# The complex product behind the scans moved from VectorE to GpSimd, with two output products a tile in place of four

## The chip, the core and the metric

The kernel runs on one core of a Trainium2 chip. Its engines work side by side, each from its own queue and in order: TensorE (PE in the profile; PEld is its loading of weights), VectorE (DVE), ScalarE (ACT), GpSimd (POOL) and SyncE (SP), which here issues most of the transfers. Engines wait for each other by semaphores. The metric is the device time of one execution in microseconds. Before the change it is 2902.01 us, the median of three runs (2901.09 to 2902.54).

## The reference

The model has two blocks. The change touches one branch of the second, a state space layer of 512 channels in 32 groups of 16, with 64 complex states in each group, over 512 tokens:

```python
def s5_branch(u, a_re, a_im, log_step, b_re, b_im, c_re, c_im, d_skip, w_glu):
    ...
    xr = jnp.einsum('blgh,gph->blgp', ug, br)
    xi = jnp.einsum('blgh,gph->blgp', ug, bi)
    ...
    _, _, sr, si = lax.associative_scan(_complex_affine_combine, (lr, li, xr, xi), axis=1)
    y = (jnp.einsum('blgp,ghp->blgh', sr, c_re.astype(f32))
         - jnp.einsum('blgp,ghp->blgh', si, c_im.astype(f32)))
    y = y.reshape(bsz, seq, SSM_WIDTH) + d_skip.astype(f32) * u32
    y = jax.nn.gelu(y).astype(u.dtype)
    ...
```

Each state obeys s[t] = lambda s[t-1] + x[t] with a complex lambda. The second branch of the same block is a forgetting attention of 8 heads; both end in the same output projection.

## The kernel before, in words

All 512 tokens lie along the free axis. The 32 groups x 64 states make 2048 states, which are 16 tiles of 128 partitions by 512 tokens; here they are called tile 0 to tile 15. The complex recurrence is done with two real scans. With lambda = mag e^(i theta), the states are first turned by e^(-i theta t), then scanned with the real factor mag, then turned back by e^(i theta t). The turning factors cos and sin are the tile `e` (halves `er` and `ei`), which SyncE loads for each state tile from HBM (L1034).

For each tile `s5_x` does this: TensorE multiplies the channels with the input matrices into two PSUM tiles (L1042, `pmm<-uT,BT`); VectorE turns them with four products that read PSUM and two sums (`w1`, `w2`, `t`); two scans follow (L1064 on `w1`, L1065 on `w2`); and four more VectorE products give er*w1, ei*w2, er*w2 and ei*w1 (`sr`, `p`, and `w2` and `w1` in place). All element operations written through the helper `tt` stand as L1056 in the profile. `s5_y` multiplies each of the four with an output matrix (L1082, `CD`; the differences are in the signs of `CD`), accumulating 32 output channels in one quarter of a PSUM tile. Tiles s and s-1 write different quarters, and their products are issued in turn. After four tiles VectorE adds the skip term (L1088).

`s5_step` runs once or twice in each half turn of the loop over pairs of attention heads: it does the output products of the tile before, then the next tile's input side, then issues the load of the next `e`. Between the steps stand the attention's projections (weights are loaded by SyncE, L108, and split into two parts by ScalarE, L114, and VectorE, L115), its norms (L1134, `qf`, and the split into `qh` and `ql`, L144 and L145), its scores (L1166 to L1170), its transposes (L1183) and the product with the values, which ends in L1203. The order on each engine comes from a scheduler, which takes instructions from different parts as they are expected to be ready; so a VectorE queue holds pieces of attention and of the state space branch in turn, and it is fixed before the run. A buffer that is reused makes its next writer wait for its last reader: `w1` and `w2` have three buffers, `sr`, `p` and `t` one, `e` two.

GpSimd has nothing to do in this part of the kernel; elsewhere it adds squares (L160), multiplies in the routing (L1467) and gathers rows.

Of the kernel before, what the change touches and what calls it, by code (L numbers as in the profile page):

```python
# [9 lines left out]
F32 = mybir.dt.float32  # L10
# [6 lines left out]
OP = mybir.AluOpType  # L17
# [54 lines left out]
def tile_kernel(ctx: ExitStack, tc: tile.TileContext, I, out, dump=None, stop=None):  # L72
    nc = tc.nc
# [10 lines left out]
    def P(name, i=None, n=1):  # L84
        o, c = _POFF[name]
        return par[:, o:o + c] if i is None else par[:, o + i:o + i + n]
# [101 lines left out]
    def scaled_split(wk, pr, g, x, hi, lo, n, bias=None):  # L188
# [4 lines left out]
        else:  # L193
# [13 lines left out]
                            in1=P("cc").rearrange("p (k t) -> p k t", t=2), op=OP.mult)  # L207
# [255 lines left out]
    for h in range(5):  # L463
# [6 lines left out]
        if h < 3:  # L470
            n = 2 * (h + 2)
# [22 lines left out]
    def tmp(bufs=3, tag="tmp", dt=F32):  # L494
        return p2.tile([128, T], dt, name=tag, tag=tag, bufs=bufs)

    def psm():
        return ps.tile([128, T], F32, name="pmm", tag="mm")
# [140 lines left out]
    for n in range(10):  # L639
        pr = psm()  # L640
        proj(pr, "w_rg", n, *hx)
        u = tmp(tag="u", bufs=3)
# [23 lines left out]
    for c in range(8):  # L666
        pu = psm()
        proj(pu, "w_u", c, *hx)
        u = tmp(tag="u", bufs=3)
        nc.scalar.activation(u, pu, GELU)  # L670
        pss = psm()
        for n in range(4):
            nc.tensor.matmul(pss[:, n * 128:(n + 1) * 128], v[n][:, c * 128:(c + 1) * 128], wst[:, c],
                             start=True, stop=True)
        y = tmp()
        nc.vector.tensor_tensor(out=y.rearrange("p (n q) -> p n q", n=4),
                                in0=pss.rearrange("p (n q) -> p n q", n=4),
                                in1=bsb[:, c:c + 1].to_broadcast([128, 4, 128]), op=OP.add)
# [7 lines left out]
    for d in range(KT):  # L686
        s5_go(N_GG)
        if d % 2 == 0:
            t = midp.tile([128, D], F32, name="thg", tag="v", bufs=4)
# [8 lines left out]
    for d in range(KT):  # L698
        pp = psm()
        proj(pp, "w_pg", d, col(ygh, 8), col(ygl, 8))  # L700
        y = tmp()
# [27 lines left out]
    s5x = ctx.enter_context(ExitStack())  # L729
    s5p = s5x.enter_context(tc.tile_pool(name="s5p", bufs=1, side="right", reuse_waits="tile"))  # L730
    BT = [s5p.tile([128, 4, 128], F32, name=f"BT{i}") for i in range(2)]
    CD = [s5p.tile([128, 16, 32], F32, name=f"CD{i}") for i in range(3)]

    def s5_mats(nc, wk):
        def tt(o, a, b, op):
            nc.vector.tensor_tensor(out=o, in0=a, in1=b, op=op)

        b1 = wk.tile([128, 16, 16], F32, name="b1")
        b2 = wk.tile([128, 16, 16], F32, name="b2")

        bre = wk.tile([128, 16, 16], F32, name="bre")
        bim = wk.tile([128, 16, 16], F32, name="bim")
        nc.scalar.dma_start(bre, I["b_re"])
        nc.scalar.dma_start(bim, I["b_im"])
        BD = [wk.tile([128, 16, 32], F32, name=f"BD{i}") for i in range(2)]
        _, cr, ci = S5C
        crb = cr.rearrange("p (s o) -> p s o", o=1).to_broadcast([128, 16, 16])
        cib = ci.rearrange("p (s o) -> p s o", o=1).to_broadcast([128, 16, 16])
        for i, (xa, xb, op) in enumerate(((bre, bim, OP.subtract), (bim, bre, OP.add))):
            nc.vector.memset(BD[i], 0.0)  # L750
            tt(b1, xa, crb, OP.mult)
            tt(b2, xb, cib, OP.mult)
            for hf in range(2):
                sl = slice(64 * hf, 64 * hf + 64)
                tt(BD[i][sl, :, 16 * hf:16 * hf + 16], b1[sl], b2[sl], op)
        cc = [wk.tile([128, 16, 16], F32, name=f"cc{i}") for i in range(2)]
        for i, n in enumerate(("c_re", "c_im")):
            nc.scalar.dma_start(cc[i], I[n])
            nc.vector.memset(CD[i], 0.0)
            for hf in range(2):  # L760
                sl = slice(64 * hf, 64 * hf + 64)
                nc.vector.tensor_scalar(CD[i][sl, :, 16 * hf:16 * hf + 16], cc[i][sl], (1.0, -1.0)[i], None, op0=OP.mult)
        nc.vector.tensor_scalar(CD[2], CD[0], -1.0, None, op0=OP.mult)
        return BD

    def s5_bt(BD, psp):
# [84 lines left out]
    o = ffn_g(0)  # L851
    for j in range(22):
        o2 = ffn_g(j + 1) if j < 21 else None
        ffn_v(j, o)
        o = o2
# [170 lines left out]
    S5 = {"n": 0, "sp": sx.enter_context(tc.tile_pool(name="sp", bufs=1, side="right", reuse_waits="tile"))}  # L1026
# [5 lines left out]
    def s5_e(s):  # L1032
        e = S5["sp"].tile([128, 2, T], F32, name="e", tag="e", bufs=2)
        nc.sync.dma_start(e.rearrange("p i t -> p (i t)"), Ed[s])  # L1034
        S5["e", s] = e[:, 0], e[:, 1]

    def s5_in(s, c):

        q, i = divmod(s, 4)
        rows = slice(32 * i, 32 * i + 32)  # L1040
        px = S5["x", s, c] = psm()
        nc.tensor.matmul(px, BT[c][rows, q], uT[rows, q], start=True, stop=True)  # L1042

    def s5_x(s):


        if s == 0:
            s5_in(0, 0)
        s5_in(s, 1)
        if s < 15:  # L1050
            s5_in(s + 1, 0)
        pxr, pxi = S5.pop(("x", s, 0)), S5.pop(("x", s, 1))
        f = lambda n, b=1: S5["sp"].tile([128, T], F32, name=n, tag=n, bufs=b)
        er, ei = S5.pop(("e", s))
        sr, t, w1, w2 = f("sr"), f("t2"), f("w1", 3), f("w2", 3)
        tt = lambda o, x, y, op: nc.vector.tensor_tensor(out=o, in0=x, in1=y, op=op)  # L1056
        tt(w1, er, pxr, OP.mult)
        tt(t, ei, pxi, OP.mult)
        tt(w1, w1, t, OP.add)
        tt(w2, er, pxi, OP.mult)  # L1060
        tt(t, ei, pxr, OP.mult)
        tt(w2, w2, t, OP.subtract)
        mb = S5C[0][:, s:s + 1].to_broadcast([128, T])
        nc.vector.tensor_tensor_scan(out=w1, data0=mb, data1=w1, initial=0.0, op0=OP.mult, op1=OP.add)  # L1064
        nc.vector.tensor_tensor_scan(out=w2, data0=mb, data1=w2, initial=0.0, op0=OP.mult, op1=OP.add)  # L1065
        p = f("p2")
        tt(sr, er, w1, OP.mult)
        tt(p, ei, w2, OP.mult)
        tt(w2, er, w2, OP.mult)
        tt(w1, ei, w1, OP.mult)  # L1070
        S5["s", s] = (sr, p, w2, w1)

    def s5_y(s):


        for n in range(2):
            for u, j in ((s, n), (s - 1, 2 + n)):
                if 0 <= u < 16:
                    q, i = divmod(u, 4)
                    if i == 0 and j == 0:  # L1080
                        S5["py", q] = psm()
                    nc.tensor.matmul(S5["py", q][32 * i:32 * i + 32], CD[(0, 2, 1, 1)[j]][:, u], S5["s", u][j],  # L1082
                                     start=j == 0, stop=j == 3)
        if s > 0:
            del S5["s", s - 1]
        q, i = divmod(s - 1, 4)
        if s > 0 and i == 3:
            nc.vector.scalar_tensor_tensor(yT[:, q], uT[:, q], P("ssm_d", q), S5.pop(("py", q)), op0=OP.mult, op1=OP.add)  # L1088

    def s5_step():  # L1090
        s = S5["n"]
        if s > 17:
            return
        if s > 0:
            s5_y(s - 1)
        if s < 16:
            s5_x(s)
        if s < 15:
            s5_e(s + 1)
        S5["n"] = s + 1  # L1100
# [130 lines left out]
    for i in range(4):  # L1231
        p = a_scores(2 * i, QK[0], QK[2])
# [12 lines left out]
        p = a_scores(2 * i + 1, QK[1], QK[3])  # L1245
# [13 lines left out]
        if i < 3:  # L1259
            v_ = a_v(i + 1)  # L1260
            QK = a_norm2(raw, rs)
            s5_step()
    while S5["n"] <= 17:
        s5_step()
    ax.close()
    dump("ys5", yT)
# [16 lines left out]
    for d in range(KT):  # L1283
        wh, wl = load_w(I["w_glu"][d].rearrange("p g k c -> p (g k c)"))
        pp = []
        for g in range(2):
            pz = psm()
            for k in range(4):
                s = slice((4 * g + k) * 128, (4 * g + k) * 128 + 128)
# [356 lines left out]
    for jg in range(NB // AJ):  # L1646
# [11 lines left out]
        for jj in range(AJ):  # L1658
            j = AJ * jg + jj
# [48 lines left out]
    for n in range(NB):  # L1708
        while len(due) < 3 and n + len(due) < NB:
            due.append(v_in(n + len(due)))  # L1710
        if 56 <= n < 56 + 8 * NTD and n % 8 == 0:
            t = n // 8 - 7
# [109 lines left out]
```

## Time and profile before

| | |
|---|---|
| median of three runs | 2902.01 us |
| the profiled execution | 2902.67 us |
| its span in the trace | 2900.9 us |
| TensorE busy | 2793.5 us, 96% |
| VectorE busy | 1976.4 us, 68% |
| ScalarE busy | 1157.0 us, 40% |
| GpSimd busy | 448.0 us, 15% |

The trace's times count from the start of the span; 1.8 us of the execution lie outside it. Busy time of TensorE is modelled, and matmuls overlap, so the distance between the starts of two matmuls says more than the duration of one. The state space tiles run from 1058 us (first input product) to 1378 us (last sum).

In the rows below, a row of the timeline has the start in us, the duration in us, the engine, the line and operation, output and inputs with their shapes, the number of instructions merged into the row, and, in brackets, how long the engine stood idle before and what ended it. A row of the groups has the number of instructions, their busy time in us and the mean of one in ns. A row of busy time by stretch has its bounds and length, then the busy us (and instructions) of PE, PEld, DVE, ACT and POOL, the granted clock, the share of the DMA engines and GB/s. A float32 product of L1082 or L1042 leaves two rows in the trace.

### The profile page before, as it was taken

Reading aid. Unit: us, or ns where it says so; the run is one execution under the profiler, and the core shown is the slowest. Engines: PE = TensorE matmul, PEld = TensorE weight load, DVE = VectorE, ACT = ScalarE, POOL = GpSimd, SP = SyncE. Lnnn points to the kernel's source line nnn. Section 1 sums busy time; section 2 is a strip of 40 time slices with the busy share of each in tenths; the row PEclk is TensorE's granted clock in tenths of the full one; section 3 lists DMA queues with packets and bytes.
Section 4 is the critical chain, followed back from the end, with each engine's and each line's share of the span. In section 5 each row is a group of like instructions: output and inputs, shape, how many; then the busy total and the mean of one; then the engine's idle time right before and its main releaser. Section 6 shows DMA issues by size and latency. Waiting matters only on the chain.

```text
span 2900.9 us, 37769 instructions
## 1 busy us (share of the span) xinstructions
PE 2793.5 (96%) x14335; PEld 2274.1 (78%) x14335; DVE 1976.4 (68%) x3569; ACT 1157.0 (40%) x1597; POOL 448.0 (15%) x470
## 2 busy tenths in 40 slices
PE   7999999999999999999999979999989999999999
PEld 4777888877888876666788879999989977777776
DVE  6786894348777686886448999998765444444444
ACT  4666523233323333434434335555543333333332
POOL 1000000010000010000000054555433122222220
PEclk9999999999999999999999989999999999999999
DMA  6333363333333332222223268989887678888884
GB/s 246 121 110 109 99 192 110 120 104 120 94 92 97 88 129 80 88 77 69 95 95 117 81 229 290 339 302 345 318 328 252 223 274 302 315 304 317 310 309 161
DMA packets 167623, 540.16 MB, mean 186 GB/s; under 512 B 16912, under 2 KB 42128, under 8 KB 163984
## 3 DMA queue, kind: packets, MB, share of 16 engines
q1 hardware_dynamic: 128272, 391.94, 40.2%
q0 software_dynamic: 36864, 134.23, 12.6%
q10 hardware_dynamic: 2304, 11.57, 1.1%
q8 instruction: 112, 1.84, 0.3%
q14 instruction: 71, 0.58, 0.1%
HBM read 479.48 MB, written 58.20 MB: 185 GB/s over the span
## 4 chain that ended last, share of the span: by engine, by line
PE 80%; DVE 9%; issue 4%; POOL 2%; ACT 2%; DMA 2%; DVEq 0%; POOLq 0%; SPq 0%; ACTq 0%
PE acc L1721 19%; PE pmm L122 16%; PE pmm L123 16%; PE pmm L124 16%; PE accg L1598 2%; DVE wlo L115 2%; POOL rows L1552 2%; DMA rows<-in_peer_u_rows_dram,idx 1%; PE pm L217 1%; PE pmm L1082 1%; PE pg L122 1%; PE pg L123 1%; PE pg L124 1%; DVE rows L1563 1%; ACT whi L114 1%
## 5 line engine op out<-in xcount | busy, mean ns | idle before, releaser
L114 ACT ACTIVATE whi<-raw 128x1024 fp32r<-128x1024 f32 (+2 forms) x502 | 517.9, 1032 | 900.4 <-PE pmm L123 724.4
L115 DVE TENSOR_TENSOR wlo<-raw,whi 128x1024 fp32r<-128x1024 f32 (+2 forms) x502 | 607.9, 1212 | 307.1 <-ACT whi L114 302.5
L124 PE MATMUL pmm<-nph,wlo 128*128 128x384 f32 (+1 forms) x1152 | 398.1, 346 | 21.5 <-DVE wlo L115 21.5
L122 PE MATMUL pmm<-nph,whi 128*128 128x384 f32 (+1 forms) x1152 | 404.8, 352 | 0.3 <-ACT whi L114 0.3
L123 PE MATMUL pmm<-npl,whi 128*128 128x384 f32 (+1 forms) x1152 | 396.9, 345 | 0.0
L145 DVE TENSOR_TENSOR wtl<-w,wth 128x384 fp32r<-128x384 f32 x128 | 71.3, 559 | 294.7 <-ACT wth L144 294.7
L1721 PE MATMUL acc<-whi,wth 128*128 128x512 f32 x768 | 244.7, 399 | 0.3 <-DVE idxT L1577 0.3
L124 PEld LDWEIGHTS pmm<-nph,wlo 128*128 128x128 f32 x1152 | 219.7, 191 | 31.3 <-DVE wlo L115 26.0
L1721 PE MATMUL acc<-wlo,wth 128*128 128x512 f32 x768 | 241.8, 396 | 0.0
L1721 PE MATMUL acc<-whi,wtl 128*128 128x512 f32 x768 | 241.2, 395 | 0.0
L144 ACT ACTIVATE wth<-w 128x384 fp32r<-128x384 f32 x128 | 67.1, 525 | 397.3 <-PE acc L1721 387.2
L122 PEld LDWEIGHTS pmm<-nph,whi 128*128 128x128 f32 x1152 | 220.3, 191 | 5.1 <-ACT whi L114 0.6
L123 PEld LDWEIGHTS pmm<-npl,whi 128*128 128x128 f32 x1152 | 220.0, 191 | 4.9 <-DVE npl L145 0.3
L1552 POOL DMA_INDIRECT rows<-in_peer_v_rows_dram,idxT x128 | 125.6, 981 | 505.2 <-PE accg L1598 402.3
L1563 DVE SCALAR_TENSOR_TENSOR rows<-rows,hN 128x1024 f32<-128x1024 f32 x128 | 155.2, 1218 | 56.2 <-DMA rows<-in_peer_u_rows_dram,idx 56.2
L1721 PEld LDWEIGHTS acc<-whi,wth 128*128 128x128 f32 x768 | 141.7, 188 | 59.5 <-ACT whi L114 26.8
L1552 POOL DMA_INDIRECT rows<-in_peer_u_rows_dram,idx x128 | 167.5, 1309 | 50.7 <-POOL rows L1551 28.3
L1721 PEld LDWEIGHTS acc<-whi,wtl 128*128 128x128 f32 x768 | 144.2, 188 | 35.5
L1721 PEld LDWEIGHTS acc<-wlo,wth 128*128 128x128 f32 x768 | 144.1, 188 | 34.7
L122 PE MATMUL pmm<-h2h,whi 128*128 128x512 f32 x352 | 137.8, 393 | 1.7 <-ACT h2h L194 1.6
L123 PE MATMUL pmm<-h2l,whi 128*128 128x512 f32 x352 | 138.6, 394 | 0.0
L124 PE MATMUL pmm<-h2h,wlo 128*128 128x512 f32 x352 | 137.9, 393 | 0.0
(543 smaller groups left out, 5800.2 us busy)
## 6 DMA issues: line engine op xcount, KB each, us to landing
raw<-in_peer_u_dram SPq DMA_DIRECT2D x128, 512.0 KB, 5.6
raw<-in_peer_v_rows_dram SPq DMA_DIRECT2D x128, 512.0 KB, 5.4
GD<-G SPq DMA_DIRECT2D x12, 2048.0 KB, 11.7
Gg<-GD SPq DMA_DIRECT2D x64, 384.0 KB, 7.2
raw<-in_w_up_dram SPq DMA_DIRECT2D x44, 512.0 KB, 3.5
AD<-act SPq DMA_DIRECT2D x48, 384.0 KB, 6.4
act<-AD SPq DMA_DIRECT2D x48, 384.0 KB, 6.6
raw<-in_w_mod_dram SPq DMA_DIRECT2D x32, 512.0 KB, 3.9
```

The lines of the kernel that those rows point to most:

```text
L114: nc.scalar.activation(hi[:, :n], raw[:, :n], AF.Copy)
L115: (eng or nc.vector).tensor_tensor(out=lo[:, :n], in0=raw[:, :n], in1=hi[:, :n].bitcast(F32), op=OP.subtract)
L122: nc.tensor.matmul(ps, wh, ah, start=first, stop=False)
L123: nc.tensor.matmul(ps, wh, al, start=False, stop=False)
L124: nc.tensor.matmul(ps, wl, ah, start=False, stop=last)
L144: nc.scalar.activation(hi, src, AF.Copy)
L145: nc.vector.tensor_tensor(out=lo, in0=src, in1=hi.bitcast(F32), op=OP.subtract)
L217: nc.tensor.matmul(pm[32 * g:32 * g + 32], cz[:, k], raw[:, j * 512:(j + 1) * 512], start=k < 4, stop=k >= 4)
L1552: nc.gpsimd.indirect_dma_start(out=r, out_offset=None, in_=I[tab], in_offset=bass.IndirectOffsetOnAxis(ap=at, axis=0))
L1563: nc.vector.scalar_tensor_tensor(r, r, 1.0, hN, op0=OP.mult, op1=OP.mult, accum_out=dot[:, n:n + 1])
L1598: nc.tensor.matmul(acc[q][32 * g:32 * g + 32], w[:, g, 31 - c:63 - c], ready[g][:, q * 512:(q + 1) * 512], start=c == 0, stop=c == 31)
L1721: nc.tensor.matmul(acc[t][q], a[:, c], bb[:, q * 512:(q + 1) * 512], start=f, stop=l)
```

## The change

The four products behind the scans go from VectorE to GpSimd, which adds two more operations: it forms the real part er*w1 - ei*w2 in `sr` and the imaginary part er*w2 + ei*w1 in `w2`. TensorE then has two output products a tile in place of four, and the third output matrix is not needed. A tile's first output product is issued two steps behind its input side (before: one step), its second three steps behind. `sr` has two buffers (before one), and `w1` two (before three).

```diff
-    CD = [s5p.tile([128, 16, 32], F32, name=f"CD{i}") for i in range(3)]
+    CD = [s5p.tile([128, 16, 32], F32, name=f"CD{i}") for i in range(2)]
...
-        nc.vector.tensor_scalar(CD[2], CD[0], -1.0, None, op0=OP.mult)
...
-        sr, t, w1, w2 = f("sr"), f("t2"), f("w1", 3), f("w2", 3)
+        sr, t, w1, w2 = f("sr", 2), f("t2"), f("w1", 2), f("w2", 3)
...
         p = f("p2")
-        tt(sr, er, w1, OP.mult)
-        tt(p, ei, w2, OP.mult)
-        tt(w2, er, w2, OP.mult)
-        tt(w1, ei, w1, OP.mult)
-        S5["s", s] = (sr, p, w2, w1)
+        gg = lambda o, x, y, op: nc.gpsimd.tensor_tensor(out=o, in0=x, in1=y, op=op)
+        gg(sr, er, w1, OP.mult)
+        gg(p, ei, w2, OP.mult)
+        gg(sr, sr, p, OP.subtract)
+        gg(w2, er, w2, OP.mult)
+        gg(w1, ei, w1, OP.mult)
+        gg(w2, w2, w1, OP.add)
+        S5["s", s] = (sr, w2)
...
-        for n in range(2):
-            for u, j in ((s, n), (s - 1, 2 + n)):
-                if 0 <= u < 16:
...
-                    nc.tensor.matmul(S5["py", q][32 * i:32 * i + 32], CD[(0, 2, 1, 1)[j]][:, u], S5["s", u][j],
-                                     start=j == 0, stop=j == 3)
+        for u, j in ((s, 0), (s - 1, 1)):
+            if 0 <= u < 16:
...
+                nc.tensor.matmul(S5["py", q][32 * i:32 * i + 32], CD[j][:, u], S5["s", u][j], start=j == 0, stop=j == 1)
...
-        if s > 17:
+        if s > 18:
             return
-        if s > 0:
-            s5_y(s - 1)
+        if s > 1:
+            s5_y(s - 2)
...
-    while S5["n"] <= 17:
+    while S5["n"] <= 18:
         s5_step()
```

The lines behind the scans shift by one to three in the changed kernel: L1055 there is L1056 here, L1063 and L1064 are the scans, L1067 is GpSimd's helper, L1084 the output products, L1135 the norm, L1170 the maxima of the scores, L1204 the product with the gate.

On GpSimd six instructions a tile are new, in this order (tile 2):

```order
L1067 TENSOR_TENSOR sr<-e,w_8565 128x512
L1067 TENSOR_TENSOR w_8565<-e,w_8565 128x512
L1067 TENSOR_TENSOR p_8575<-e,w_8566 128x512
L1067 TENSOR_TENSOR sr<-sr,p_8575 128x512
L1067 TENSOR_TENSOR w_8566<-e,w_8566 128x512
L1067 TENSOR_TENSOR w_8566<-w_8566,w_8565 128x512
```

The scheduler has put ei*w1 second; the last of the six is the last reader of `w1`.

On VectorE, before the first norm of queries and keys, tile 2 (`w_8568` is its w1, `w_8569` its w2) stands as follows before:

```order
L1056 TENSOR_TENSOR t_8567<-e,pmm 128x512
L1056 TENSOR_TENSOR w_8569<-e,pmm 128x512
L1056 TENSOR_TENSOR w_8568<-w_8568,t_8567 128x512
L115 TENSOR_TENSOR wlo<-raw,whi 128x1024
L1056 TENSOR_TENSOR t_8567<-e,pmm 128x512
L1064 SCALAR_TENSOR_TENSOR w_8568<-mag,w_8568 128x512
L1056 TENSOR_TENSOR w_8569<-w_8569,t_8567 128x512
L1056 TENSOR_TENSOR sr<-e,w_8568 128x512
L1065 SCALAR_TENSOR_TENSOR w_8569<-mag,w_8569 128x512
L1056 TENSOR_TENSOR w_8568<-e,w_8568 128x512
L1056 TENSOR_TENSOR p_8578<-e,w_8569 128x512
L1134 SCALAR_TENSOR_TENSOR qf<-pmm,qg,qf 128x512
```

and in the changed kernel (`w_8565` and `w_8566` are tile 2's w1 and w2, `w_8768` is tile 3's w1):

```order
L115 TENSOR_TENSOR wlo<-raw,whi 128x1024
L1055 TENSOR_TENSOR t_8564<-e,pmm 128x512
L1055 TENSOR_TENSOR w_8566<-e,pmm 128x512
L1055 TENSOR_TENSOR w_8565<-w_8565,t_8564 128x512
L1055 TENSOR_TENSOR w_8768<-e,pmm 128x512
L1055 TENSOR_TENSOR t_8564<-e,pmm 128x512
L1063 SCALAR_TENSOR_TENSOR w_8565<-mag,w_8565 128x512
L1055 TENSOR_TENSOR w_8566<-w_8566,t_8564 128x512
L1064 SCALAR_TENSOR_TENSOR w_8566<-mag,w_8566 128x512
L115 TENSOR_TENSOR wlo<-raw,whi 128x1024
L1135 SCALAR_TENSOR_TENSOR qf<-pmm,qg,qf 128x512
L1135 SCALAR_TENSOR_TENSOR qf<-pmm,par,qf 128x512
```

Three products went from between the scan and the norm, one split of weights (L115) came in behind the second scan, and the first product of the next tile came in ahead of the first scan.

On VectorE the close pair of tiles 13 and 14 is the other place. Before, tile 14 (`w_10219` is its w1, `w_10220` its w2, `w_10372` is tile 15's w1) stands so:

```order
L1056 TENSOR_TENSOR t_10218<-e,pmm 128x512
L1056 TENSOR_TENSOR w_10220<-e,pmm 128x512
L1056 TENSOR_TENSOR w_10219<-w_10219,t_10218 128x512
L1056 TENSOR_TENSOR w_10372<-e,pmm 128x512
L1056 TENSOR_TENSOR t_10218<-e,pmm 128x512
L1064 SCALAR_TENSOR_TENSOR w_10219<-mag,w_10219 128x512
L1056 TENSOR_TENSOR w_10220<-w_10220,t_10218 128x512
L1056 TENSOR_TENSOR sr<-e,w_10219 128x512
L1065 SCALAR_TENSOR_TENSOR w_10220<-mag,w_10220 128x512
L1056 TENSOR_TENSOR w_10219<-e,w_10219 128x512
L1056 TENSOR_TENSOR p_10229<-e,w_10220 128x512
```

and in the changed kernel (`w_10216` and `w_10217` are tile 14's, `w_10369` is tile 15's w1):

```order
L1055 TENSOR_TENSOR t_10215<-e,pmm 128x512
L1055 TENSOR_TENSOR w_10217<-e,pmm 128x512
L1055 TENSOR_TENSOR w_10216<-w_10216,t_10215 128x512
L1055 TENSOR_TENSOR w_10369<-e,pmm 128x512
L1055 TENSOR_TENSOR t_10215<-e,pmm 128x512
L1063 SCALAR_TENSOR_TENSOR w_10216<-mag,w_10216 128x512
L1055 TENSOR_TENSOR w_10217<-w_10217,t_10215 128x512
L1204 SCALAR_TENSOR_TENSOR m_8029<-tha,pmm 128x512
L1064 SCALAR_TENSOR_TENSOR w_10217<-mag,w_10217 128x512
L1170 TENSOR_REDUCE nmax<-pmm 128x1 x4
```

The gate's product (L1204) and the maxima moved ahead of, and directly behind, the second scan. Tile 15's w1 stands at the same place as before, ahead of tile 14's first scan, but with two buffers it now takes the buffer of tile 13.

## Rows read from the trace of the kernel before

**Rows 1.** Busy time by stretch, 1055 to 1380 us.

```profile
1055.00:1380.00 325.00, 315.79 (x1588) 214.18 (x1586) 248.89 (x396) 131.56 (x233) 0.00 (x0) 0.99 0.27 88
```

**Rows 2.** The chain of waits in 1055 to 1390 us, its shares by line.

```profile
by line: PE pmm L122 16.3%; PE pmm L123 15.5%; PE pmm L124 14.9%; PE pmm L1082 7.1%; DVE w L1056 4.9%; DVE wlo L115 4.6%; PE pmm L1149 4.1%; PE pmm L1151 4.0%; PE pmm L1150 4.0%; PE pmm L1042 3.1%; DVE t L1056 2.8%; ACT whi L114 2.5%; DVE w
```

**Rows 3.** Timeline of TensorE: output products of two steps.

```profile
1162.77 1.90 PE L1082 MATMUL pmm<-w,CD 128*32 128x512 f32 x4
...
1188.28 0.62 PE L1082 MATMUL pmm<-sr,CD 128*32 128x512 f32 x1
...
1190.12 1.13 PE L1042 MATMUL pmm<-uT,BT 32*128 32x512 f32 x4
```

**Rows 4.** Waits in 1055 to 1380 us: the sum in us, times, the longest.

```profile
PE pmm L1082 <- DVE p L1056: 2.3, 3, 1.3
```

**Rows 5.** Groups of VectorE's instructions, 1055 to 1380 us.

```profile
L1056 DVE TENSOR_TENSOR w<-e,w 128x512 f32<-128x512 f32 x32 | 21.5, 674 | 0.0
...
L1056 DVE TENSOR_TENSOR sr<-e,w 128x512 f32<-128x512 f32 x16 | 10.9, 684 | 0.0
```

**Rows 6.** Timeline: GpSimd's and VectorE's sums of squares.

```profile
1020.50 1.29 POOL L160 TENSOR_TENSOR sa<-sa,sq 128x512 f32<-128x512 f32 x1 [2.23 <-ACT sq L159]
1021.06 1.27 DVE L160 TENSOR_TENSOR sb<-sb,sq 128x512 f32<-128x512 f32 x1 [0.64 <-ACT sq L159]
...
1031.78 0.69 DVE L160 TENSOR_TENSOR sb<-sb,sq 128x512 f32<-128x512 f32 x1
```

**Rows 7.** Timeline: a GpSimd product in the routing, and VectorE beside it.

```profile
1801.66 1.21 DVE L1465 TENSOR_TENSOR eq<-fa,iof 128x1024 f32<-128x1024 f32 x1
1802.80 0.68 DVE L1522 TENSOR_TENSOR oa<-o,GH 128x1024 f16<-128x1024 f16 x1
1802.96 2.79 POOL L1467 TENSOR_TENSOR eq<-eq,idf 128x1024 f32<-128x1024 f32 x1 [3.87 <-DVE eq L1465]
...
1803.40 2.89 DVE L1522 TENSOR_TENSOR ob<-o,GL 128x1024 f16<-128x1024 f16 x1
```

**Rows 8.** Timeline: GpSimd's sums beside VectorE products with one operand in PSUM.

```profile
16.20 4.84 POOL L160 TENSOR_TENSOR sc<-sc,sqc 128x256 f32<-128x256 f32 x6 [2.10 <-ACT sqc L159]
...
19.19 4.87 DVE L265 TENSOR_TENSOR xt<-xt,pr 128x512 f32<-128x512 f32 x8 [1.32 <-PE pr L185]
```

**Rows 9.** GpSimd's groups over the span.

```profile
L160 POOL TENSOR_TENSOR s<-s,sq 128x512 f32<-128x512 f32 x6 | 10.3, 1712 | 489.2 <-ACT sq L159 489.2
```

**Rows 10.** Timeline of VectorE: tiles 3 and 4, then tiles 13 and 14.

```profile
1149.39 1.22 DVE L1064 TENSOR_TENSOR_SCAN w<-mag,w 128x512 f32<-128x512 f32 x1
...
1159.96 1.22 DVE L1064 TENSOR_TENSOR_SCAN w<-mag,w 128x512 f32<-128x512 f32 x1
...
1315.78 1.22 DVE L1064 TENSOR_TENSOR_SCAN w<-mag,w 128x512 f32<-128x512 f32 x1
1322.61 2.35 DVE L115 TENSOR_TENSOR wlo<-raw,whi 128x1024 fp32r<-128x1024 f32 x2
...
1327.87 1.22 DVE L1064 TENSOR_TENSOR_SCAN w<-mag,w 128x512 f32<-128x512 f32 x1
...
1332.52 0.68 DVE L1203 SCALAR_TENSOR_TENSOR m<-tha,pmm 128x512 f32<-128x512 f32 x1
```

**Rows 11.** The chain of waits before the first scores, in order of time.

```profile
1117.96 0.59 DVE t L1056
...
1126.13 0.66 DVE qf L1134
...
1127.39 0.67 DVE qf L1134
```

**Rows 12.** ScalarE's loads of function tables for the branch's gelu.

```profile
L1278 ACT ACT_TABLE_LOAD x4 | 5.1, 1283 | 0.1
```

**Rows 13.** Timeline of SyncE: a load of `e`, and the landing of such loads.

```profile
1155.20 0.33 SPq L1034 DMA_DIRECT2D e<-Ed  x1
...
DMA to landing us min/median/max: 3.1/3.3/5.3
```

More of the change, by code (lines that the diff above doesn't have):

```diff
@@ L1066, in s5_x @@
         p = f("p2")
-        tt(sr, er, w1, OP.mult)
-        tt(p, ei, w2, OP.mult)
-        tt(w2, er, w2, OP.mult)
-        tt(w1, ei, w1, OP.mult)
-        S5["s", s] = (sr, p, w2, w1)
-    def s5_y(s):
-        for n in range(2):
-            for u, j in ((s, n), (s - 1, 2 + n)):
-                if 0 <= u < 16:
-                    q, i = divmod(u, 4)
-                    if i == 0 and j == 0:
-                        S5["py", q] = psm()
-                    nc.tensor.matmul(S5["py", q][32 * i:32 * i + 32], CD[(0, 2, 1, 1)[j]][:, u], S5["s", u][j],
-                                     start=j == 0, stop=j == 3)
+        gg = lambda o, x, y, op: nc.gpsimd.tensor_tensor(out=o, in0=x, in1=y, op=op)
[6 more added lines that the diff above has]
+        S5["s", s] = (sr, w2)
+    def s5_y(s):
+        for u, j in ((s, 0), (s - 1, 1)):
+            if 0 <= u < 16:
+                q, i = divmod(u, 4)
+                if i == 0 and j == 0:
+                    S5["py", q] = psm()
+                nc.tensor.matmul(S5["py", q][32 * i:32 * i + 32], CD[j][:, u], S5["s", u][j], start=j == 0, stop=j == 1)
         if s > 0:
```

## The prediction

> **What bounds the kernel now.** I read three views of the stretch in which the state space tiles run: busy time by stretch, the chain of waits, and the timelines of TensorE and VectorE.
>
> Busy time [rows 1] shows TensorE at 315.79 of 325 us at a granted clock of 0.99, VectorE at 248.89 us (77%), GpSimd at nothing. The chain of waits [rows 2] says the same with names: the products of the attention (L122 to L124, L1149 to L1151) lead it, the output products L1082 alone have 7.1%, which is 0.071 x 335 = 23.8 us, and VectorE's products, sums and weight splits named there have 4.9 + 4.6 + 2.8 = 12.3%, or 41 us. So a microsecond that VectorE gains or loses in this stretch reaches the end at about 41 / 248.89 = 0.165, and one that TensorE saves in L1082 counts where L1082 stands on the chain. The three places where a state space tile itself sets the pace are a TensorE wait for the product `p` [rows 4], the close pairs of tiles [rows 10], and the first norm of queries and keys [rows 11].
>
> **TensorE's part.** L1082 issues four products a step before and two after, 64 in place of 32 over 16 tiles. A step of four runs from 1188.28 to 1190.12, 1.84 us [rows 3]; at 1162.77 two products without a partner from the other tile leave four records and take 1.90, so products gain by running in pairs, and a step that keeps its pairs costs 0.92. On the chain this halves 23.8 us: **-11.9 us**. If all of it were on the critical path, it would be 17 steps, some of them split in two groups of that length as at 1162.77, so about 20 x 1.84 = 36.8 us halved: -18.4, the lower bound. Above, it can't be nothing, since the chain of rows 2 is 12.3% VectorE and the rest mostly TensorE.
>
> TensorE also waits three times for `p`, 2.3 us together [rows 4]. A first output product now comes two steps behind; the closest tiles stand 10.6 us apart [rows 10], so two steps are at least 21 us, and GpSimd's six operations (below, 9 to 16 us) are done. These waits go; the longest, 1.27, falls to a close pair and is counted there. **-1.2** here, with -2.3 as the bound.
>
> **VectorE's part.** 64 products leave it. One is recorded at 0.674 to 0.684 us [rows 5], and records overlap by 0.07 (1801.66 with 1.21, the next at 1802.80 [rows 7]), so 64 x 0.61 = 39 us. What may take their place is waiting. Where GpSimd and VectorE both read two operands from SBUF, VectorE's 0.69 became 1.27 beside a GpSimd operation of 1.29 [rows 6]; and beside one of 2.79 VectorE's second operation lasted 2.89, while the one that began just before GpSimd's kept its 0.68 [rows 7]. Eight products with an operand in PSUM ran at 4.87 / 8 = 0.61 beside GpSimd's work [rows 8], undisturbed. So one GpSimd operation of this size holds VectorE for about 1.2 us (2.79 less its own wait of half a microsecond, halved, gives 1.15; rows 6 give 1.29), but only the operations without a PSUM operand: the sum before each scan, the scans, the weight splits L115, the splits `ql`. No row shows a scan beside GpSimd. I take it as held, since it reads an SBUF tile and a broadcast column; if it isn't, the first norm and the pairs each lose a wait or two, and the sum is some 3 us lower.
>
> The Trainium skill, in SBUF — State Buffer, section Who interferes with whom, states this as an exclusive lock for a whole instruction, between a GpSimd instruction that reads SBUF and a VectorE one with two SBUF inputs; rows 6 to 8 agree. By it scans are held too, which no row here shows, and the sum stays at the upper of these two readings.
>
> Between the ends: 96 operations that each hold VectorE for 1.2 would give 115 - 39 = +76 us of VectorE, none held gives -39. In a tile's list (the change's rows), GpSimd starts behind the first scan; the sum and second scan and one L115 or `ql` follow there, the rest is PSUM work or idle time. Three held a tile, 48 x 1.2 = 58, net +19, times 0.165 = +3.1. I price the places one by one, and they come to the same:
>
> - First norm. From the first `t` at 1117.96 to `qf` at 1126.13 is 8.2 us before [rows 11]. After, in the order shown, it is six operations of 0.6 (3.6), two scans at 1.14 and a split at 1.14 (7.0), plus two waits for GpSimd of 1.25: 9.5. The second `qf` follows at once (0.66 in place of 1.26), so it is +0.7 late. Behind it the `ql` splits wait for the last operations of tile 2, twice 1.25, of which 0.4 is covered by TensorE's earlier work: +2.1. Together **+2.8**; bounds -1.8 (no waits, 7.0 against 8.2 and the shorter pair) and +5.5 (two more waits).
> - The norms behind tiles 6 and 11 stand at the same distance from two scans, with a weight split beside GpSimd's end: some +0.8 each, **+1.6** (0 to 3).
> - Close pairs, 3-4, 8-9 and 13-14. The first product of tile s+2 is placed ahead of tile s+1's first scan, and with two buffers of `w1` it waits for GpSimd's last operation on tile s. GpSimd's chain from the first scan's end: six at 1.2 is 7.2, the sum (0.6) and second scan (1.14) that it waits for 1.7, then up to three operations of VectorE that get in between: 9 to 12. With scan 1.2 in front and two products 1.2 behind, a pair is 11.5 to 14.4 apart, against 10.57 and 12.09 before [rows 10]. That is late by about 2.5. Against it, `m` (L1204) stands behind the sum now: from the scan's start 1.8 in place of 4.65 (1332.52 - 1327.87 [rows 10]), 2.85 earlier, and the maxima follow. Net -0.2 to -0.5 for each of the three: **-1.1** (bounds -5 if GpSimd takes 9, +8 if 15).
>
> **The rest.** One more table load stands around the branch's gelu (55 for 54 in all), 1.283 us [rows 12]; ScalarE is half covered there: **+0.6** (0 to 1.3). The load of `e` waits for GpSimd's fifth operation in place of VectorE's last, some 3 us later; before it was issued at 1155.20 and lands within 5.3 at most [rows 13], and its use comes a step or more later, so it hides, and the weight loads queued behind it on SP keep four buffers of lead. If not, a step waits 1 to 2 us. The small product for the third `CD` leaves VectorE (0.4 us, in an earlier part where TensorE works): nothing.
>
> **Sum.** -11.9 - 1.2 + 2.8 + 1.6 - 1.1 + 0.6 = -9.2. The profiled execution took 2902.67 (its span and 1.8 outside), so 2893.5; it was 0.66 above the median of the runs: **2892.8**. What is late next is TensorE's projections again.
>
> **Rivals.** By 0.2% (5.8 us), about what a measurement can tell, same is 2896.2 to 2907.8.
>
> 1. *TensorE counts everywhere, VectorE is hardly held.* -18.4 - 2.3, scans not held: 2902.0 - 20.7 + 0.6 = 2882. For it: TensorE busy 97% of the stretch. Against: rows 2 give L1082 only 7.1%, and rows 6 and 7 the holding. 0.12.
> 2. *VectorE gains nothing and loses what TensorE wins.* Each GpSimd operation holds VectorE for 1.2: +76 x 0.165 = +12.6, so 2902.0 - 11.9 + 12.6 + 0.6 = 2903, no change. For it: rows 6 and 7 show whole operations lost; VectorE at 77% finds something to be held nearly always. Against: much of its queue reads PSUM, as rows 8. 0.24. The Trainium skill, in Perfetto Trace Analysis, section Optimizing Scalar/DVE Operations, warns that offloading between these two might not help since they share a read port; this is that rival.
> 3. *Slower: GpSimd is slow here, and holds VectorE.* Six sums that began beside VectorE's work averaged 1.712 [rows 9]. If its products take that and hold VectorE throughout, it is 96 x 1.71 = 164 - 39 = +125, x 0.165 = +20.7: 2902.0 - 11.9 + 20.7 + 0.6 = 2911; the place is the close pairs, where GpSimd's chain passes 15 us and `w1` comes late. It decides from (11.9 + 5.8 - 0.6) / 0.165 = 104 us of VectorE net, or 143 / 96 = 1.49 held per operation. Against: 1.29 undisturbed [rows 6]. 0.16.
> 4. *The change doesn't do what it says*: TensorE waits for GpSimd in place of `p`. It needs a chain longer than 21 us a tile; 0.02, near rival 2.
>
> **Numbers.** The forecast has 0.46, its own range 2885 to 2898. With the ends of rivals 1 and 3 cut off, 2881 to 2909. Faster: rival 1's 0.12 and 0.42 of the forecast, 0.54; same: rivals 2 and 4 and the forecast's upper end, 0.30; slower: rival 3, 0.16.
>
> **What would show it.** Right: L1084 with about half its share of the chain and no wait for GpSimd; GpSimd busy some 120 to 160 us in the stretch; second scans at 2.3 in place of 1.22, L115 at up to 2.4; VectorE idle, released by GpSimd, ahead of a product at tiles 5, 10 and 15; the stretch shorter by some 9 us. Wrong: scans at 1.22 throughout (rival 1), VectorE above 300 us busy (2), GpSimd above 1.5 an operation with waits at every step (3).

## The result and the profile after

The changed kernel takes 2924.96 us, the median of four runs (2920.07 to 2926.37), against 2901.55 us before (four runs, 2897.05 to 2902.54): a ratio of 1.0081, 95% interval 1.0063 to 1.0098. It is slower by 23.4 us, where 2892.8 was forecast, in a range that ended at 2909.

The same stretch as in [rows 1], 20 us longer because the changed kernel needs longer for it (start and length, then busy us and instructions of TensorE, its weight loads, VectorE, ScalarE, GpSimd; the granted clock, the DMA share, GB/s):

```profile
1055.00:1400.00 345.00, 316.38 (x1499) 220.28 (x1497) 237.67 (x327) 129.38 (x229) 154.46 (x96) 0.90 0.24 79
```

GpSimd is busy for 154 us, inside the 120 to 160 expected, and VectorE has less to do. What stands out is the clock: 0.99 before [rows 1], 0.90 now. A mean of 0.90 between full speed (2.4 GHz) and half (1.2 GHz) means some 345 x 0.10 x 2 = 69 us at half speed, time in which TensorE waits at that clock included.

The chain of waits from 1055 to 1410 us, by line, and then the waits from 1055 to 1400 us (engine and line, what it waited for, us in all, times, the longest), to set beside [rows 2, 4]:

```profile
by line: PE pmm L122 13.0%; PE pmm L123 12.4%; PE pmm L124 11.7%; issue 5.1%; DVE wlo L115 4.1%; POOL w L1067 4.1%; PE pmm L1084 4.0%; POOL sr L1067 3.9%; DMA e<-Ed 3.7%; PE pmm L1150 3.2%; PE pmm L1152 3.1%; PE pmm L1151 3.1%; DVE w L1055 
```

```profile
DVE w L1055 <- DMA e<-Ed: 18.1, 5, 6.2
...
PE pmm L122 <- DVE t L1055: 9.5, 3, 3.9
...
PE pmm L122 <- ACT qh L144: 6.3, 4, 4.0
PE pmm L123 <- DVE ql L145: 5.8, 2, 2.9
...
PE pmm L1006 <- DVE fl L1001: 4.3, 1, 4.3
```

The output products fell from 7.1% to 4.0% of the chain, as forecast, and TensorE's waits for `p` are gone. In their place stand GpSimd's two groups (4.1 and 3.9%) and a load that was said to hide: VectorE waits 18.1 us for `e`. TensorE has seven waits of 1.8 to 4.3 us that were not there before: one at the forget gates, three at the norms (after tiles 2, 6, 11), three at the close pairs.

This is the first close pair in the timeline (tiles 3 and 4): GpSimd's last two operations on tile 3, SyncE's load of `e`, VectorE's product that needs it, TensorE behind it. In brackets, the idle time before and what ended it.

```profile
1167.14 1.27 POOL L1067 TENSOR_TENSOR w<-e,w 128x512 f32<-128x512 f32 x1
1168.49 1.27 POOL L1067 TENSOR_TENSOR w<-w,w 128x512 f32<-128x512 f32 x1
...
1168.44 0.33 SPq L1033 DMA_DIRECT2D e<-Ed  x1
...
1172.21 0.69 DVE L1055 TENSOR_TENSOR w<-e,pmm 128x512 f32<-128x512 f32 x1 [6.17 <-DMA e<-Ed]
...
1173.55 0.58 PE L122 MATMUL pmm<-qh 128*128 128x256 f32 x1 [3.90 <-DVE t L1055]
```

GpSimd's fifth operation ends at 1168.41 and only then can the load be issued. VectorE's product is the first of tile 5, which the order has put ahead of tile 4's first scan, and it needs tile 5's `e`, in the buffer that tile 3 has just left. It starts at 1172.21; GpSimd had given back `w1` at 1169.76, 2.45 us earlier. So the wait that I forecast for `w1` is there, and a longer one for `e` hides it. TensorE idles 3.90 us, and before it starts again the clock has fallen:

```profile
1165.00:1170.00 5.00, 4.66 (x27) 2.77 (x26) 1.04 (x2) 0.00 (x0) 4.61 (x4) 1.00 0.12 19
1170.00:1175.00 5.00, 1.45 (x5) 0.84 (x5) 2.79 (x4) 0.00 (x0) 0.23 (x1) 0.67 0.48 191
1175.00:1180.00 5.00, 4.45 (x12) 3.36 (x12) 4.00 (x7) 1.90 (x7) 4.84 (x4) 0.50 0.00 0
1180.00:1185.00 5.00, 5.00 (x20) 4.04 (x19) 0.18 (x1) 2.95 (x7) 3.62 (x3) 0.81 0.32 102
1185.00:1190.00 5.00, 5.00 (x24) 3.83 (x24) 1.23 (x1) 1.59 (x4) 0.00 (x0) 1.00 0.29 108
```

TensorE works again from 1173.55, but at 0.50: 12 matrix products in the 5 us from 1175, and 24 in the 5 us after the clock is back at 1.00. Each of the seven waits has such a stretch at its end.

At the first norm the holding of VectorE is plain (second scan, weight split, three `ql` splits, and TensorE's first score product):

```profile
1125.23 2.19 DVE L1064 TENSOR_TENSOR_SCAN w<-mag,w 128x512 f32<-128x512 f32 x1
1127.34 2.22 DVE L115 TENSOR_TENSOR wlo<-raw,whi 128x1024 fp32r<-128x1024 f32 x1
...
1131.46 4.51 DVE L145 TENSOR_TENSOR ql<-qf,qh 128x512 fp32r<-128x512 f32 x3
...
1131.59 1.54 PE L122 MATMUL pmm<-qh 128*128 128x512 f32 x4 [3.98 <-ACT qh L144]
```

Undisturbed, the scan and the split take 1.22 [rows 10]. Over all tiles, in the groups of the stretch (instructions, busy us, mean ns):

```profile
L1067 POOL TENSOR_TENSOR w<-e,w 128x512 f32<-128x512 f32 x32 | 54.6, 1707 | 1.3
...
L1064 DVE TENSOR_TENSOR_SCAN w<-mag,w 128x512 f32<-128x512 f32 x16 | 29.1, 1821 | 0.1
```

### The profile page after: what moved, and what is told of

Its sections match the earlier page's. It is cut to its first block, busy times and chain, and to the rows that moved or that the text cites. A ratio compares the mean times of both kernels' runs of the same rounds, so it can differ in the third digit from the quotient of the medians.

```text
span 2918.1 us, 37708 instructions
## 1 busy us (share of the span) xinstructions
PE 2793.9 (96%) x14271; PEld 2280.4 (78%) x14271; DVE 1965.8 (67%) x3504; ACT 1159.9 (40%) x1598; POOL 605.5 (21%) x566
## 3 DMA queue, kind: packets, MB, share of 16 engines
q8 instruction: 111, 1.82, 0.3%
## 4 chain that ended last, share of the span: by engine, by line
PE 76%; DVE 11%; issue 6%; POOL 4%; ACT 2%; DMA 1%; POOLq 0%; DVEq 0%; ACTq 0%
PE acc L1722 19%; PE pmm L122 15%; PE pmm L123 15%; PE pmm L124 14%; DVE wlo L115 2%; PE accg L1599 2%; POOL rows L1553 2%; DVE rows L1564 1%; POOL rows L1552 1%; PE pm L217 1%; PE pg L122 1%; PE pg L123 1%; PE pg L124 1%; DMA raw<-in_w_mod_dram 1%; POOL w L1067 0%
## 5 line engine op out<-in xcount | busy, mean ns | idle before, releaser
L115 DVE TENSOR_TENSOR wlo<-raw,whi 128x1024 fp32r<-128x1024 f32 (+2 forms) x502 | 614.5, 1225 | 311.3 <-ACT whi L114 306.5
```

Source lines behind the costliest of these rows:

```text
L115: (eng or nc.vector).tensor_tensor(out=lo[:, :n], in0=raw[:, :n], in1=hi[:, :n].bitcast(F32), op=OP.subtract)
```

## Experiments

Three theories. **E**: the load of `e`, released late by GpSimd and needed early by the product put ahead of the scan, and behind it `w1` (the expectations call `w1` alone W). **L**: GpSimd holds VectorE's scans and splits, TensorE waits for them. **U**, formed later: the output products that went away had covered TensorE's waits. Common to all is what a wait costs: its length and the half speed that comes with it. In the expectations of the later runs, P says that the loss is made at those seven places, S that it is made everywhere in proportion. The last column is the granted clock over 1055 to 1400 us.

| run | median, us | ratio to before | 95% interval | clock |
|---|---|---|---|---|
| changed kernel | 2925.0 | 1.0081 | 1.0063 to 1.0098 | 0.90 |
| w13: three `w1` | 2922.3 | 1.0079 | 1.0060 to 1.0097 | 0.91 |
| ec: `e` loaded once | 2913.1 | 1.0044 | 1.0031 to 1.0057 | 0.92 |
| ec_w13: both | 2903.4 | 1.0009 | 0.9999 to 1.0019 | 0.95 |
| es_w13: both, with real loads | 2909.9 | 1.0033 | 1.0024 to 1.0042 | 0.96 |
| nogp: no complex product | 2883.8 | 0.9943 | 0.9928 to 0.9958 | 0.97 |
| nogp4: the same, four output products | 2891.4 | 0.9969 | 0.9959 to 0.9980 | 0.99 |
| junk: nogp and unread GpSimd work | 2907.6 | 1.0023 | 1.0013 to 1.0032 | 0.92 |
| dve6: all six on VectorE | 2902.6 | 1.0006 | 0.9996 to 1.0017 | 0.96 |
| mix: sums only on GpSimd | 2916.9 | 1.0055 | 1.0042 to 1.0067 | 0.93 |
| hyb: nine tiles on GpSimd | 2896.6 | 0.9985 | 0.9976 to 0.9995 | 0.96 |
| hyb1b: eight, as before elsewhere | 2897.2 | 0.9987 | 0.9977 to 0.9996 | 0.99 |
| g5: five | 2890.2 | 0.9965 | 0.9953 to 0.9978 | 1.00 |

**What the close pairs wait for: w13, ec, ec_w13, es_w13.**

```diff
 w13:
-        sr, t, w1, w2 = f("sr", 2), f("t2"), f("w1", 2), f("w2", 3)
+        sr, t, w1, w2 = f("sr", 2), f("t2"), f("w1", 3), f("w2", 3)
 ec (ec_w13: both edits):
-        e = S5["sp"].tile([128, 2, T], F32, name="e", tag="e", bufs=2)
-        nc.sync.dma_start(e.rearrange("p i t -> p (i t)"), Ed[s])
+        e = S5["e1"] = S5["e1"] if s else S5["sp"].tile([128, 2, T], F32, name="e", tag="e", bufs=1)
+        s or nc.sync.dma_start(e.rearrange("p i t -> p (i t)"), Ed[s])
```

Expected of w13: 

> The changed kernel with three buffers of w1 in place of two, and the same order on every engine. Theory E (the load of e, which GpSimd now releases late and which the hoisted first product of a tile needs, ends the wait at the close pairs; in the changed kernel's trace e lands 2.0 to 2.5 us after GpSimd's last operation): no change, 2925 within 4, and VectorE still waits for e some 18 us. Theory W (the two buffers of w1, as the prediction had it): VectorE's waits at the close pairs shrink by 4 us each and the time falls to 2912 or less. Theory L (GpSimd holding VectorE's scans and splits is the whole cost): no change too.

Expected of ec: 

> The changed kernel with e loaded once and kept for all tiles, so tiles 1 to 15 are turned by tile 0's factors: 15 loads of 512 KB are left out; w1 still has two buffers. Theory E: VectorE's waits at the close pairs (6.2, 4.5, 4.5 us) end 2.0 to 2.5 us earlier, at GpSimd's last operation, TensorE's waits there fall from 3.9, 1.8, 3.8 to about 1.5, 0, 1.7, and some of the clock's falls behind them go: 2912 to 2918. Theory W: the same waits as before the edit, 2925 within 4. Theory L: 2925 within 4.

Expected of ec_w13: 

> e loaded once (tiles 1 to 15 use tile 0's factors) and three buffers of w1. Theory E with W behind it: the three close pairs don't wait at all, TensorE's 9.5 us of waits there go and so do three stretches of 10, 3 and 10 us at a granted clock of 0.5 to 0.6, worth up to half their length: 2903 to 2910. Theory L: 2920 or more, since GpSimd's holding of VectorE is untouched.

A third `w1` alone changes nothing that can be measured; VectorE still waits 18.0 us for `e`. With `e` loaded once the time falls to 2913.1, and the wait that was hidden comes up (waits of ec):

```profile
DVE w L1055 <- POOL w L1067: 8.8, 3, 3.8
```

With both it is 2903.4, with no wait of VectorE at the pairs. Theory E is shown in its order, `e` first and `w1` second, about 12 and 10 us in these runs, which also leave out 15 of the 16 loads; W alone, which was my forecast's mechanism, fell.

es_w13 asks for the same with the loads kept:

```diff
-        e = S5["sp"].tile([128, 2, T], F32, name="e", tag="e", bufs=2)
-        nc.sync.dma_start(e.rearrange("p i t -> p (i t)"), Ed[s])
-        S5["e", s] = e[:, 0], e[:, 1]
+        er = S5["sp"].tile([128, T], F32, name="er", tag="er", bufs=3)
+        ei = S5["sp"].tile([128, T], F32, name="ei", tag="ei", bufs=2)
+        nc.sync.dma_start(er, Ed[s][:, 0:T])
+        nc.sync.dma_start(ei, Ed[s][:, T:2 * T])
+        S5["e", s] = er, ei
...
-        s2 = f2("qs", 2)
+        s2 = f2("qs", 1)
```

Expected of es_w13: 

> The changed kernel with cos and sin loaded as two tiles, three buffers of cos (which the hoisted product reads) and two of sin, three of w1, and one buffer in place of two of the norm's squares to make room. If the late e and then w1 are what the pairs wait for, it comes to what the run with e loaded once and three w1 gave, 2903, give or take 5, though each load is now two of 256 KB. If the single load of e helped for another reason (less traffic, fewer entries in SyncE's queue): 2910 or more.

It gives 2909.9, between the two answers. TensorE's waits at the close pairs are gone in its trace, so late buffers were the cause there; but 6.5 us against ec_w13 remain, and whether they come from the traffic, the doubled loads or the norm's single buffer was not separated. By this run the buffers are worth 15 us of the changed kernel's time, by ec_w13 21.5.

**What GpSimd's work costs where nobody waits for it: nogp, nogp4, junk.**

```diff
 nogp:
-        gg(sr, er, w1, OP.mult)
...
-        gg(w2, w2, w1, OP.add)
-        S5["s", s] = (sr, w2)
+        S5["s", s] = (w1, w2)
 junk, beside that and the single e:
+        gg(sr, er, w1, OP.mult)
+        gg(p, er, sr, OP.mult)
+        gg(sr, ei, p, OP.mult)
...
 nogp4, beside nogp:
+        for n in range(2):
+            for u, j in ((s, n), (s - 1, 2 + n)):
...
+                    nc.tensor.matmul(S5["py", q][32 * i:32 * i + 32], CD[j % 2][:, u], S5["s", u][j // 2], start=j == 0, stop=j == 3)
```

Expected of nogp: 

> No complex product behind the scans at all: the output products read w1 and w2 as the scans leave them (the four products and two sums of each tile are left out), with the changed kernel's two output products a tile, two and three steps behind, w1 with three buffers. Theory E plus L: neither the late e nor the holding is left, also TensorE's waits of 4.0, 2.9, 2.9 at the norms and the clock's falls behind them go: 2880 to 2892, that is the output products' 12 us below the kernel before, and a few more for VectorE's 39. Rival (the later output products or the new order are at fault, not GpSimd): above 2905.

Expected of junk: 

> The run without the complex product (the output products read w1 and w2 as scanned), with six GpSimd operations of 128x512 in each tile added whose results nobody reads, the first started by the first scan; e is loaded once (tiles 1 to 15 use tile 0's factors), w1 has three buffers. Nothing waits for GpSimd, so what it costs against the run without them (2884) is its holding of VectorE alone. Theory L (held VectorE, then TensorE's waits and the clock's fall): 2898 to 2908, as the run with one e and three w1 (2903), scans at about 1.8 us, and a granted clock of 0.5 behind the waits at the gates and norms. Rival (the rest of the loss came from waiting for GpSimd's results): 2880 to 2888.

Expected of nogp4: 

> The run without the complex product (2884), with four output products a tile in place of two (w1 and w2 each read twice), two and three steps behind. The prediction's term: the 32 products are on the critical path for 12 us of their 18, so 2896, give or take 3. Rival U (the products covered TensorE's waits at the norms; without them the wait grows past a microsecond and the clock falls, 24 us at half speed in that run against 7 before): the four products give cover back, the granted clock stays at 1.0 around the norms behind tiles 6 and 11, and it is 2884 to 2891.

Without the complex product it is 2883.8: TensorE's part of the change and the later output products are no loss. Six GpSimd operations a tile whose results nobody reads bring it to 2907.6, 23.9 us more, and TensorE's waits at the gates and the first norm are back, with the half speed behind them (junk, timeline of TensorE, then busy time by stretch):

```profile
1086.10 0.59 PE L1006 MATMUL pmm<-fl,tri 128*128 128x8 f32 x2 [5.38 <-DVE fl L1001]
...
1137.56 1.54 PE L122 MATMUL pmm<-qh 128*128 128x512 f32 x4 [3.98 <-ACT qh L144]
```

```profile
1130.00:1140.00 10.00, 6.02 (x26) 3.30 (x24) 9.97 (x9) 4.83 (x6) 8.88 (x6) 0.84 0.18 58
1140.00:1150.00 10.00, 10.00 (x29) 5.22 (x29) 5.32 (x9) 5.03 (x13) 1.36 (x1) 0.50 0.00 0
```

That is theory L by itself; no buffer and no result is waited for. Against nogp, ec_w13 gives the same term as 19.7.

nogp4 measures the forecast's TensorE term: four products cost 7.6 us over two, not 12. Its clock tells why. In nogp, TensorE waits 1.18 us for `ql` at the norm behind tile 6, and the clock falls; in nogp4 the products stand in that place and the wait is 0.6 (nogp's timeline and busy time, then nogp4's):

```profile
1201.73 0.50 PE L123 MATMUL pmm<-ql,qh 128*128 128x512 f32 x1 [1.18 <-DVE ql L145]
```

```profile
1200.00:1202.00 2.00, 0.76 (x2) 0.45 (x3) 2.00 (x4) 0.01 (x1) 0.00 (x0) 1.00 0.59 184
1202.00:1204.00 2.00, 2.00 (x8) 0.92 (x7) 2.00 (x4) 1.58 (x3) 0.00 (x0) 0.76 0.50 197
1204.00:1206.00 2.00, 2.00 (x8) 1.00 (x8) 2.00 (x5) 0.96 (x1) 0.00 (x0) 0.50 0.00 0
```

```profile
PE pmm L123 <- DVE ql L145: 1.2, 2, 0.6
```

```profile
1200.00:1210.00 10.00, 9.39 (x53) 4.33 (x51) 8.45 (x13) 6.15 (x8) 0.00 (x0) 1.00 0.35 107
```

By the clock, nogp spends 345 x 0.03 x 2 = 21 us at half speed and nogp4 7; 14 us at half speed are some 7 us of work lost again, an estimate. Theory U holds as an effect, but doesn't eat all: nogp is still the faster one, and nogp4's 2891.4 lies 0.4 above what U allowed (2884 to 2891), below the 2893 to 2899 of the forecast's term.

**Which engine the products and sums suit: dve6, mix.**

```diff
 dve6:
-        gg = lambda o, x, y, op: nc.gpsimd.tensor_tensor(out=o, in0=x, in1=y, op=op)
+        gg = lambda o, x, y, op: nc.vector.tensor_tensor(out=o, in0=x, in1=y, op=op)
 mix (gg on GpSimd):
+        tt(sr, er, w1, OP.mult)
+        tt(p, ei, w2, OP.mult)
+        tt(w2, er, w2, OP.mult)
+        tt(w1, ei, w1, OP.mult)
+        gg(sr, sr, p, OP.subtract)
+        gg(w2, w2, w1, OP.add)
```

Expected of dve6: 

> All six operations of each tile on VectorE, two output products a tile, two and three steps behind; no GpSimd. VectorE has 32 operations more than in the kernel before (19.5 us), none is held, and e and w1 come free early. By the chain's shares: 2901 - 12 (output products) - 2 (waits for p) + 19.5 x 0.165 = 2890; 2885 to 2896. Rival (VectorE's work is what bounds the norms and pairs, so each added operation there counts in full and the clock falls behind it): 2900 to 2910.

Expected of mix: 

> The four products on VectorE as in the kernel before, only the two sums of each tile on GpSimd; two output products a tile. e is free as early as before; GpSimd's 32 operations of 1.3 come last in a tile. Theory P: e doesn't wait, GpSimd's two operations still fall beside the ql splits at the norms, so two or three of TensorE's waits stay, smaller: 2889 to 2898. Theory S: VectorE as loaded as before and held 32 x 1.2 = 38 us more, x 0.165 = 6: 2895; the trace tells them apart by where TensorE waits.

Both expectations of mine missed. dve6 comes out even with the kernel before, as the rival said. At the first norm TensorE waits 1.82 us for VectorE's sum `sr`, where it waited 0.66 for `p` before, and 1.82 for `qh` at the norm behind tile 6, where its longest wait was 0.56; the clock is 0.96. That these sums and the half speed pay back all of TensorE's gain is argued. mix is 14 us slower still, though VectorE has 32 operations fewer than in dve6. At the first norm (mix, timeline of VectorE and TensorE):

```profile
1132.12 1.38 DVE L1055 TENSOR_TENSOR w<-e,w 128x512 f32<-128x512 f32 x1
...
1134.88 1.54 PE L122 MATMUL pmm<-qh 128*128 128x512 f32 x4 [3.84 <-ACT qh L144]
```

One product between the two `qf` is held for 0.7 us by GpSimd's first sum, and the output products which TensorE did in that gap before (between waits of 0.66 and 1.53) are no longer there: a wait of 3.84. So U and L add at one place. That these two make up the whole 14 us was not separated.

**Whether the place decides: hyb, hyb1b, g5.**

```diff
 hyb, from the changed kernel:
+        gg = lambda o, x, y, op: (nc.vector if s in (0, 2, 3, 6, 8, 11, 13) else nc.gpsimd).tensor_tensor(out=o, in0=x, in1=y, op=op)
 hyb1b, from the kernel before (g5: in (4, 7, 9, 12, 14)):
+        g = s in (4, 5, 7, 9, 10, 12, 14, 15)
+        gg = lambda o, x, y, op: (nc.gpsimd if g else nc.vector).tensor_tensor(out=o, in0=x, in1=y, op=op)
...
+        if g:
+            gg(sr, sr, p, OP.subtract)
...
+        S5["s", s] = (sr, None, w2, None) if g else (sr, p, w2, w1)
```

Expected of hyb: 

> The changed kernel (two output products a tile, two buffers of w1 and of e) with the six operations of tiles 0, 2, 3, 6, 8, 11 and 13 on VectorE and those of the other nine on GpSimd. Those seven are the ones whose GpSimd operations stand beside TensorE's seven waits in the changed kernel's trace (forget gates, three norms, three close pairs). Theory P (the loss is made at these places: late e at the pairs, held VectorE at the norms and the gates, and the clock's fall behind each): the waits go, VectorE pays 7 x 6 x 0.61 = 26 us of work of which 0.165 reaches the end, 4 us: 2886 to 2896, below the kernel before. Rival S (GpSimd's holding costs VectorE everywhere in proportion): 9 of 16 tiles keep it, so some 2925 - 7/16 x 41 = 2907.

Expected of hyb1b: 

> The kernel before, with only tiles 4, 5, 7, 9, 10, 12, 14 and 15 given to GpSimd (six operations, two output products each); the other eight keep four VectorE products and four output products, and all output products stay one and two steps behind, so the norms and close pairs are as before. By the sum: TensorE half of 12, so -6; VectorE 8 x 4 x 0.61 = 20 us less and 8 x 3 x 1.2 = 29 held, +1.5: 2896, and 2890 if the eight places have room for the holding. Rival (GpSimd's holding costs TensorE waits at any place, as in the run with only the sums on GpSimd): 2902 to 2912.

Expected of g5: 

> As the run with eight tiles on GpSimd and output products one and two steps behind (2897), but with five: 4, 7, 9, 12 and 14. In that run's trace TensorE waited three times for GpSimd's sr, 1.9 to 2.9 us, at tiles 5, 10 and 15, whose next step follows too soon; these three now stay on VectorE. If those waits (6.7 us, and 3 us at half speed behind them) were what kept the gain small, they go, against three tiles' gain of about 1 us each: 2890 to 2895. If GpSimd's holding takes back what each tile gains wherever it runs: 2897 to 2901.

hyb has 54 of the 96 operations on GpSimd and is faster than before (0.9985), 0.6 us outside the forecast's upper end: the loss is made at the places named, not in proportion. At the first norm it has dve6's wait of 1.82 us, and it has 14 and 10 us at half speed at the other two; that this is what keeps it there is argued. hyb1b leaves norms and pairs as before, but its output products come one step behind, and TensorE waits for GpSimd there:

```profile
PE pmm L1089 <- POOL sr L1068: 6.7, 3, 2.9
```

Those three were tiles 5, 10 and 15. g5 takes them back to VectorE: no such wait, 3.4 us at half speed in the whole stretch (1084 to 1088, clock 0.57 there; 7 before), and 2890.2 us, a ratio of 0.9965. It beats both kernels with 30 operations on GpSimd.

## Why the prediction was wrong

The mechanisms were mostly named; what failed was three steps and one omission, and -9.2 became +23.4. Measured by the runs in turn, each a step from the last: nogp4 against before -9.3 (VectorE's 64 products gone, nothing held), nogp -7.6 (two output products), ec_w13 +19.7 (GpSimd's work), ec +9.7 (`w1`), changed kernel +11.9 (`e`). They come to 24.3 by construction, since each run is set against the next; that is no check on the single steps. The last three are rough: nogp keeps the loads of `e` that ec_w13 and ec leave out. With the loads, es_w13 gives 26.1 for GpSimd's work and 15.1 for the two buffers together.

- **"so it hides"** (the load of `e`) failed, and with it the sum. I saw that the first product of tile s+2 now stands ahead of tile s+1's scan and followed its buffer `w1`, but `e` is the other operand of the same product, and has two buffers as well; its release is followed by a load of 3.3 us [rows 13], so here it comes after `w1`. Before, the load was issued at 1155.20 [rows 13] for a use at 1168.05, the first line below; here issue at 1168.44, use blocked until 1172.21. The term, 0, was +11.9 (this and the next together 6.5 less by the run with real loads).
- **The close pairs, -1.1**, were +9.7 by themselves. GpSimd's chain was sized rightly: 9 to 12 forecast, and from the first scan's end at 1159.2 to 1169.8 it is 10.6. The gain set against it, `m` standing 2.85 earlier, can't show while the scan ahead of it waits.
- **GpSimd's holding**, +2.8 and +1.6 at the norms in the sum, was 19.7 to 23.9 in the runs. The first norm was sized about right: `qf` comes 9.1 us after `t` (9.5 forecast), and TensorE's wait grows from 1.53 to 3.98, by 2.45. The norms behind tiles 6 and 11 were not: the waits grow from 0.6 to 2.9, by 2.3 each, against 0.8 in the sum (last two lines below). The gates, at tile 0, I had left out altogether: 4.29. So the waits alone were some 11 us in place of 4.4, and no term had the half speed behind them. The single hold of a second scan was smaller than forecast, 1.82 in the mean against 2.3. The factor 0.165, which the places were checked against, is an average over the stretch; the holds fall just behind the scans, where norms and gates wait for VectorE.
- **The omission**: each wait was priced at its own length. A wait of TensorE of 1.2 to 4.3 us comes here with 3 to 14 us at half speed. The seven make 69 us at half speed, against 7 before. In some 9 of the 69 TensorE still waits; the other 60 cost 30 us, an estimate, beside 23.6 for the waits themselves. No term had it, though [rows 1] show the clock at 0.99, which was there to lose.
- **TensorE, -11.9 and -1.2** (the second is 1.0 by its own rows, 2.3 - 1.27), measured -7.6 for the products. About half the chain's share of L1084 went, as forecast, but the products had been cover for the waits at the norms.
- Rival 3, the slow side, forecast 2911 with the close pairs as its place, by GpSimd taking 1.71 an operation. It averaged 154.46 / 96 = 1.61, and the pairs made 15 to 21.5 us of the loss, but through `e` first; the deciding point of 104 us of VectorE's time was the wrong measure, since VectorE ended less busy than before.

From the kernel before, the first product of tile 5 and TensorE's waits at the norms:

```profile
1168.05 0.68 DVE L1056 TENSOR_TENSOR w<-e,pmm 128x512 f32<-128x512 f32 x1
```

```profile
PE pmm L122 <- ACT qh L144: 1.9, 2, 1.5
PE pmm L123 <- DVE ql L145: 1.1, 2, 0.6
```

## What to carry to other kernels

When an operation moves to a slower engine, list every buffer that it reads and what refills it: here the operand with a load behind it came back later than the one in plain sight. Price a new wait of TensorE with the half speed that comes with it, and count output products or other filler that the change takes away as cover. Work on GpSimd beside two-operand VectorE work is cheap only where nothing behind those operations is awaited: five tiles of sixteen gained, sixteen lost.

## What the runs showed of the hardware that was not expected

VectorE was held in casts with a single SBUF operand too, and an instruction of one element a partition was held as long. At tiles 0 and 1 of the changed kernel, beside GpSimd:

```profile
1063.28 1.25 DVE L953 CAST identb<-ident 128x128 bf16<-128x128 f32 x1
...
1065.83 1.24 DVE L960 TENSOR_TENSOR selq<-ident 128x1 f32<-128x1 f32 x1
...
1087.12 1.25 DVE L1013 CAST fc<-fc 128x32 bf16<-128x32 f32 x1
```

Before they took 0.20, 0.15 and 0.17 us. The first two, with the second scan, a `tensor_scalar` and two more `selq`, lost 1.0 to 1.1 us each and made the forget gates late: the copy `fx` that they start from comes 12.6 us after tile 0's first scan starts, 7.4 before. The third comes behind TensorE's wait at the gates. The Trainium skill, in SBUF — State Buffer, section Who interferes with whom, says that copies and casts can enter a mode with both port pairs, where their operands allow it, and then contend with GpSimd; the trace agrees that these casts were held, with these numbers, and doesn't show the mode.

GpSimd is held in turn: its second operation took 2.08 at 1161.00 beside the second scan, against 1.27 to 1.30 for the same form alone. And the clock fell in nogp behind a wait of 1.18 us at a norm, while in the kernel before it stayed at 1.00 behind one of 1.53 at another: the length of one wait doesn't tell it. And no wait of TensorE stands in front of the fall at 1084 in g5, where it had run the gates' products of 128x8.
